# Scores that start 24 and 28 slots after their loads, and stores to scratch issued by ScalarE, in a hybrid attention and RG-LRU layer

## The chip, the cores and the metric

The kernel runs on one core of a Trainium2 chip. The metric is the device time of one execution in microseconds; lower is better. The core has a matrix engine (TensorE, "PE" in the profile, its weight loads "PEld"), a vector engine (VectorE, "DVE"), a scalar engine (ScalarE, "ACT"), a general engine (GpSimd, "POOL") and a queue engine that only issues transfers (SyncE, "SP"). Each engine runs its own instructions strictly in order and waits for the others on semaphores. Transfers (DMAs) run on 16 shared DMA engines; SP and ACT can issue them.

## What is computed

One decoder layer on 1024 positions of width 2048, in float32:

```
h = rms_norm(x, norm_gain)
q, k, v, g_attn, xr, g_rec = split(h @ w_in)         # 6 x 1024 columns
q, k = rope(q), rope(k)                              # 8 heads, 2 maps of 64 each
p = softmax(causal(q k^T / 8));  w = p[0] - lam * p[1]
o = rms_norm(w @ v, subln_gain) * (1 - lam_init) * silu(g_attn)
r = causal_conv(xr);  r = rg_lru(r) * silu(g_rec)    # 8 blocks of 128
x = x + concat(o, r) @ w_out
out = rms_norm(x, final_gain)
```

## The kernel before

The 1024 positions are worked off in two halves of 512 (`b` or `l` = 0 and 1). In each half, 16 units come in the order of `UNITS`: eight attention heads and eight recurrent blocks. A head unit makes four projections (the two halves of q and k, then v, then the gate), a recurrent unit two. One projection is 48 matmuls of 128x512 (16 row tiles of the input, 3 products each: every float32 operand is split into a high and a low part and high x high, high x low and low x high are added up); these are the matmuls of line 367. After the 16 units of a half comes the output projection (line 826).

Around this stream of projections the program places everything else by **slots**. The class `Slots` counts them: `tick()` moves the count by one, and generators (`stream`, `loader`, `scores`, `weighted`, `rope`, `values`, `lru`, `head_out`, stores) yield the number of slots until they go on. One slot passes for every three matmuls of a projection. So a `yield 4` puts what follows 12 matmuls later in TensorE's order. Slots set the order in which instructions are recorded, not times.

The weights come through `stream`: each 256 KB tile is loaded by SP into a raw buffer, ACT rounds it into the high part (line 169), POOL or DVE takes the low part (line 170). Buffers of 128x512 come from one pool of 89, first freed, first used again.

A head's way from projection to scores goes through scratch memory in HBM. When the second projection (pb) is done, DVE multiplies it by cosine and sine, `rope` subtracts and adds, splits into high and low, and four stores of 256 KB write the parts into the scratch tensor `fs`, whose first dimension has length 4 (each store has the shape 4 x 32 x 512). Then `head_load` reads it back in another arrangement: two k tiles (128x512) and four q tiles, each q tile a 64x512 block that is read twice (shape 2 x 64 x 512). In the second half also the k and v tiles of the first half are loaded. `scores` takes the head's tiles and issues, per block of 128 query rows, the score matmuls (line 632 with the high q, line 633 with the low q), the mask and maximum on DVE, the exponentials on ACT and the combination of both maps on DVE. `weighted` transposes the weights (line 755) and multiplies them with v (lines 777 to 780), `head_out` normalises.

Before the change, all transfers are issued by SP, through `load` (line 155) and `store` (line 159). The scores start three slots after their loads are recorded (`yield 3` in `scores`), and the loads are recorded one slot after the stores at the earliest (`yield 1` in `rope`).

In the texts below T0 is the moment at which TensorE finishes pb of a head.

Of the kernel before, what the change touches and what calls it, by code (L numbers as in the profile page):

```python
# [55 lines left out]
UNITS = ("h0", "h1", "r0", "h2", "r1", "h3", "r2", "h4", "r3", "h5", "r4", "h6", "h7", "r5", "r6",  # L56
         "r7")
ORDER = (0, 1, 2, 3, 4, 8, 9, 10, 11, 12, 5, 6, 13, 14, 7, 15)
SCORE_STEP = 2
SCORE_PACE = (4, 4)  # L60
TURN_PACE = 2
# [2 lines left out]
class Slots:  # L64


    def __init__(self):
        self.now = 0
        self.seq = 0
        self.tasks = []  # L70
# [36 lines left out]
class Trunk:  # L107
    def __init__(self, ctx, tc, io):
        self.tc = tc
        self.nc = tc.nc  # L110
        self.io = io
        e = ctx.enter_context
        self.cst = e(tc.tile_pool(name="cst", bufs=1))
        self.dram = e(tc.tile_pool(name="scr", bufs=1, space=bass.MemoryType.DRAM))
        self.bp = e(tc.tile_pool(name="buf", bufs=1))
        self.ps = e(tc.tile_pool(name="ps", bufs=1, space=bass.MemoryType.PSUM))
        self.tr, self.av, *self.dense = [
            self.ps.tile([P, HALF], F32, name=f"pq{i}") for i in range(4)]
        self.swide = [self.ps.tile([P, 1024], F32, name=f"sw{i}") for i in range(2)]
        self.n = 0  # L120
        self.sl = Slots()
        self.free = deque(range(NB))
        self.wide = [self.bp.tile([P, 1024], F32, name=f"wide{i}") for i in range(5)]
        self.avbusy = self.trbusy = False
        self.cur = self.phase = 0
        self.rsb, self.sin, self.cos, self.tabs, self.Y = {}, {}, {}, {}, {}
        self.fs, self.vsc, self.vnow, self.gate, self.rgate, self.msc = {}, {}, {}, {}, {}, {}
        self.ready, self.hd, self.es = set(), {}, {}
        self.scored, self.flipped, self.weighed = [], 0, 0

    def nm(self, s):
# [24 lines left out]

    def store(self, dst, b, delay=3, record=None, keep=False):
        def go():
            self.nc.sync.dma_start(dst, b.f)
            if record:  # L160
                record[0][record[1]] = dst
            if not keep:
                self.rel(b)
            return
            yield
        self.sl.spawn(go(), delay)
# [75 lines left out]
    def weights(self):  # L242
        io = self.io
        for b in range(2):
# [7 lines left out]
            yield from (io["w_in"][u, g] for u in us for g in range(4))  # L252
            yield from (io["w_out"][cg, kt] for cg in range(4) for kt in ORDER)

# [204 lines left out]
    def rope(self, b, h, ts):  # L459
        nc = self.nc  # L460
        t1, t2, t3, t4 = ts
        self.tt(t1.f, t1.f, t2.f, ALU.subtract)
        self.tt(t3.f, t3.f, t4.f, ALU.add)
        yield 1
        self.split(t1.f, t2, t1)
        self.split(t3.f, t4, t3)
        yield 4
        fs = self.dram.tile([4, 4, 32, HALF], F32, name=self.nm("fs"))
        for i, t in enumerate((t2, t4, t1, t3)):
            self.load(fs[:, i], t.f)  # L470
        self.rel(*ts)
        self.fs[h, b] = fs
        yield 1
        self.ready.add(("q", h, b))

    def values(self, b, h, vt):
        nc = self.nc
        yield 2
        while not self.settled():
            yield 1  # L480
        o = self.spare()
        for i in range(4):
            nc.tensor.transpose(o[:, i * P:(i + 1) * P], vt.f[:, i * P:(i + 1) * P], self.ident)  # L483
        vh, vl = self.allocr(), self.allocr()
        self.split(o, vh, vl)
        self.rel(vt)
        self.vnow[h] = (vh, vl)
        if b == 0:
            self.vsc[h] = (self.scratch("vs"), self.scratch("vs"))
            yield 4  # L490
            for d, t in zip(self.vsc[h], (vh, vl)):
                self.load(d, t.f)
        self.ready.add(("v", h, b))


# [88 lines left out]
    def head_load(self, h, l):  # L584
        k, q, v = [], [], []
        for c in range(l + 1):
            ks = []
            for m in range(2):
                kk = self.allocr()
                self.load(kk.f, self.fs[h, c][2 + m].rearrange("i r c -> (i r) c"))  # L590
                ks.append(kk)
            k.append(ks)
        for i in (0, 2):
            for m in range(2):
                t = self.allocr()
                src = self.fs[h, l][m, i:i + 2].rearrange("i r c -> (i r) c")
                self.load(t.f, src.unsqueeze(0).broadcast_to([2, 64, HALF]))
                q.append(t)
        if l:
            vs = []  # L600
            for d in self.vsc[h]:
                t = self.allocr()
                self.load(t.f, d)
                vs.append(t)
            v.append(vs)
        self.hd[h, l] = (k, q, v)

    def loader(self):
        for l in range(2):
            for h in range(NH):  # L610
                while (("q", h, l) not in self.ready or 8 * l + h - self.weighed > 1
                       or len(self.free) < FREE_HEAD):
                    yield 1
                self.head_load(h, l)
                yield 1

    def score(self, h, l, j, p0, es):
# [8 lines left out]
        for m in range(2):  # L626
            st = self.swide[m]
            for c in range((cols + 511) // 512):
# [4 lines left out]
                nc.tensor.matmul(o, lhsT=q[2 + m].r[:, qs], rhs=kk, start=False, stop=True)  # L633
        yield SCORE_STEP
        for m in range(2):
# [4 lines left out]
        nc.vector.tensor_scalar_mul(mx, mx, -(QK ** -0.5))  # L640
        yield SCORE_STEP
        p1 = self.wide[3]
        for m, p in enumerate((p0, p1)):
            nc.scalar.activation(p[:, :cols], self.swide[m][:, :cols], AF.Exp, scale=QK ** -0.5,  # L644
                                 bias=mx[:, m:m + 1], accum_out=sm[:, m:m + 1])
        yield SCORE_STEP
        nc.vector.tensor_tensor(out=es[:, j:j + 1], in0=sm[:, 0:1], in1=sm[:, 0:1], op=ALU.mult)
# [8 lines left out]
    def scores(self):  # L656
        n = 0
        for l in range(2):
            for h in range(NH):
                while (h, l) not in self.hd:  # L660
                    yield 1
                yield 3
                es = self.cst.tile([P, 4], F32, name=self.nm("es"), tag="es", bufs=4)
                self.es[h, l] = es
                for j in range(4):
                    while n - 2 * self.flipped > 3:
                        yield 1
                    p0 = self.wide[(0, 1, 2, 4)[n % 4]]
                    n += 1
                    yield from self.score(h, l, j, p0, es)  # L670
                    self.scored.append(p0)
                    yield SCORE_PACE[l]
                k, q, v = self.hd[h, l]
                self.rel(*q, *(t for ks in k for t in ks))
# [118 lines left out]
    def outputs(self, b):  # L793
# [10 lines left out]
        for cg in range(4):  # L804
            for i, kt in enumerate(ORDER):
                while cg == 0 and len(raws) + len(mixes) < min(KT, i + 5):
                    raws.append(self.mix(ORDER[len(raws) + len(mixes)], b))
                while cg == 0 and len(mixes) < min(KT, i + 2):
                    x, hi, lo = raws.popleft(), self.allocr(), self.allocr()
                    mixes[ORDER[len(mixes)]] = (hi, lo)  # L810
                    self.split(x.f, hi, lo)
# [55 lines left out]
            self.rel(y)  # L867

    def run(self):
        engines = {mybir.EngineType.PE, mybir.EngineType.SP}  # L870
        if True:
            self.consts()
            for gen in (self.stream(), self.loader(), self.scores(), self.weighted()):
                self.sl.spawn(gen)
            for b in range(2):
                for name in UNITS:
                    (self.head if name[0] == "h" else self.rec)(b, int(name[1]))
                self.final(b)
                self.outputs(b)
# [58 lines left out]
```

## Time and profile before

| | |
|---|---|
| time, median of 3 runs | 2202.98 us (2202.58 to 2203.88) |
| time of the profiled execution | 2201.42 us |
| its span, first to last instruction | 2199.6 us |
| TensorE busy | 1739.8 us (79%) |
| mean granted TensorE clock | 0.883 of full |
| ACT, POOL, DVE busy | 793.6, 858.7, 761.4 us |
| DMA engines' busy share (queue 1) | 34.2% |

A row of waits says which engine and line waited for what, and in how many pieces. The chain of waits follows the work that ended last back in time. In a table of windows the DMA share is the mean busy share of 16 DMA engines, so one engine alone is 0.0625. A "PEclk" of 0.50 is the lower of TensorE's two clocks (1.2 GHz) and 1.00 the higher (2.4 GHz). "b" is a buffer of the pool, "fs", "vs" and "ms" are scratch tensors in HBM (rotated q and k; v of the first half; gated outputs), "pq" and "sw" PSUM tiles.

### The profile page before, as it was taken

The numbers are of one execution on the slowest core, as the hardware profiler recorded it, in microseconds if no ns is written. First come the engines' busy times: TensorE is split into PE (matmuls) and PEld (weight loads), VectorE is DVE, ScalarE is ACT, GpSimd is POOL, SyncE is SP. The second block draws the span as 40 slices with busy tenths as digits, with TensorE's granted clock in tenths as the row PEclk, the third lists the DMA queues.
The fourth block names the chain that finished last, engine by engine and source line by source line (L and its number), as shares of the span: only waits on it lengthen the run. The fifth ranks groups of instructions, "written<-read, shape, count | busy, mean of one in ns | idle before, by whom it ended". The sixth has DMA issues, their size and how long they took to land. (4 is left out here: it accounts for less than half of the span.)

```text
span 2199.6 us, 22066 instructions
## 1 busy us (share of the span) xinstructions
PE 1739.8 (79%) x7716; PEld 1409.8 (64%) x7716; DVE 761.4 (35%) x1333; ACT 793.6 (36%) x1383; POOL 858.7 (39%) x710
## 2 busy tenths in 40 slices
PE   7568695959595869989957786959595958689996
PEld 5357474748484657778846675848484847577885
DVE  8334141515141335740223433324232424346001
ACT  6215151515151326642413342424251513266221
POOL 7313433424251325766613142415151513256560
PEclk9779897979797979999979897979797979799998
DMA  5423323233322234523723142423232323245422
GB/s 200 136 78 99 108 82 105 85 102 99 100 91 87 87 120 150 163 67 122 255 81 107 56 131 64 120 69 116 74 115 74 103 84 99 91 131 188 117 78 77
DMA packets 131503, 237.03 MB, mean 108 GB/s; under 512 B 13248, under 2 KB 17472, under 8 KB 131392
## 3 DMA queue, kind: packets, MB, share of 16 engines
q1 hardware_dynamic: 131392, 235.63, 34.2%
q8 instruction: 60, 0.98, 0.2%
q14 instruction: 51, 0.42, 0.1%
HBM read 197.83 MB, written 37.75 MB: 107 GB/s over the span
## 5 line engine op out<-in xcount | busy, mean ns | idle before, releaser
L367 PE MATMUL pq<-b,b 128*128 128x512 f32 x4512 | 1162.4, 410 | 17.2 <-ACT b L169 8.0
L170 POOL TENSOR_TENSOR b<-b,b 128x512 fp32r<-128x512 f32 x504 | 678.2, 1359 | 990.3 <-ACT b L169 706.6
L367 PEld LDWEIGHTS pq<-b,b 128*128 128x128 f32 x4512 | 877.5, 199 | 195.1 <-ACT b L169 8.5
L169 ACT CAST b<-b 128x512 fp32r<-128x512 f32 x592 | 349.7, 618 | 848.5 <-PE pq L367 219.6
L632 PE MATMUL sw<-b,b 128*128 128x512 f32 (+2 forms) x192 | 78.1, 408 | 278.1 <-DMA b<-fs 277.8
L173 DVE TENSOR_TENSOR b<-pq,b 128x512 f32<-128x512 f32 x113 | 75.1, 687 | 525.9 <-PE pq L367 434.6
L632 PEld LDWEIGHTS sw<-b,b 128*128 128x128 f32 x192 | 42.2, 220 | 296.3 <-issue 169.1
L637 DVE CUSTOM_DVE_ANT_0 sw<-sw,mask 128x128 f32<-128x128 f32 (+7 forms) x128 | 96.6, 770 | 376.2 <-PE sw L633 375.9
L826 PE MATMUL pq<-b,b 128*128 128x512 f32 x768 | 198.2, 393 | 5.0 <-DVE wide L173 5.0
L826 PE MATMUL sw<-b,b 128*128 128x512 f32 x768 | 196.3, 391 | 0.0
L826 PEld LDWEIGHTS pq<-b,b 128*128 128x128 f32 x768 | 144.9, 189 | 37.0 <-DVE wide L173 5.9
L826 PEld LDWEIGHTS sw<-b,b 128*128 128x128 f32 x768 | 145.3, 189 | 30.5
L173 POOL TENSOR_TENSOR b<-b,b 128x512 f32<-128x512 f32 (+1 forms) x98 | 129.4, 1325 | 89.8 <-ACT b L548 31.6
L633 PE MATMUL sw<-b,b 128*128 128x512 f32 (+2 forms) x192 | 77.1, 407 | 103.0 <-DMA b<-fs 103.0
L633 PEld LDWEIGHTS sw<-b,b 128*128 128x128 f32 x192 | 40.8, 212 | 126.8 <-DMA b<-fs 120.5
L644 ACT ACTIVATE wide<-sw,mx 128x128 f32<-128x128 f32 (+7 forms) x128 | 93.8, 738 | 67.0 <-DVE mx L640 66.2
L170 DVE TENSOR_TENSOR b<-b,b 128x512 fp32r<-128x512 f32 x88 | 92.1, 1071 | 32.5 <-ACT b L169 25.7
L169 ACT CAST b<-pq 128x512 fp32r<-128x512 f32 x16 | 9.4, 587 | 253.3 <-PE pq L483 253.3
L763 POOL MEMSET b<- 128x128 f32 x64 | 12.9, 205 | 185.0 <-PE pq L367 181.3
L764 ACT CAST b<-pq 128x512 fp32r<-128x512 f32 (+1 forms) x80 | 43.4, 542 | 108.5 <-PE pq L755 108.5
L765 DVE TENSOR_TENSOR b<-pq,b 128x512 fp32r<-128x512 f32 (+1 forms) x80 | 50.7, 634 | 45.1 <-ACT b L764 37.7
L755 PE MATMUL pq<-ident,wide 128*128 128x128 f32 x288 | 52.1, 286 | 17.6 <-DVE wide L652 16.8
(130 smaller groups left out, 1345.3 us busy)
## 6 DMA issues: line engine op xcount, KB each, us to landing
b<-w_in SPq DMA_DIRECT2D x384, 256.0 KB
b<-w_out SPq DMA_DIRECT2D x128, 256.0 KB
b<-fs SPq DMA_DIRECT2D x112, 256.0 KB
fs<-b SPq DMA_DIRECT2D x64, 256.0 KB
b<-xt SPq DMA_DIRECT2D x32, 256.0 KB
ms<-b SPq DMA_DIRECT2D x32, 256.0 KB
b<-ms SPq DMA_DIRECT2D x32, 256.0 KB
wide<-x SPq DMA_DIRECT2D x20, 256.0 KB
```

The source lines that it names most:

```text
L169: self.nc.scalar.copy(hi.r, x)
L170: (eng or self.nc.vector).tensor_tensor(out=lo.r, in0=x, in1=hi.f, op=ALU.subtract)
L173: (eng or self.nc.vector).tensor_tensor(out=out, in0=a, in1=b, op=op)
L367: self.nc.tensor.matmul(acc, lhsT=x.r[:, s], rhs=y.r, start=kt == 0 and j == 0, stop=kt == KT - 1 and j == 2)
L632: nc.tensor.matmul(o, lhsT=q[m].r[:, qs], rhs=kk, start=True, stop=False)
L633: nc.tensor.matmul(o, lhsT=q[2 + m].r[:, qs], rhs=kk, start=False, stop=True)
L637: nc.vector.tensor_tensor_reduce(out=s, in0=s, in1=self.mask[:, 896 - off:896 - off + cols], scale=1.0, scalar=NEG, op0=ALU.add, op1=ALU.m ...
L644: nc.scalar.activation(p[:, :cols], self.swide[m][:, :cols], AF.Exp, scale=QK ** -0.5, bias=mx[:, m:m + 1], accum_out=sm[:, m:m + 1])
L755: nc.tensor.transpose(self.tr[:, c:c + P], ws[qi][:, kb * P:(kb + 1) * P], self.ident)
L764: nc.scalar.copy(wh.r[:, first:], self.tr[:, first:])
L765: nc.vector.tensor_tensor(out=wl.r[:, first:], in0=self.tr[:, first:], in1=wh.f[:, first:], op=ALU.subtract)
L826: nc.tensor.matmul(accs[t], lhsT=x.r[:, s], rhs=z.r, start=i == 0 and j == 0, stop=i == KT - 1 and j == 2)
```

## The change

Three edits go together. The scores of a head now start 24 slots (first half) or 28 slots (second half) after its loads were recorded, instead of 3. In `rope` the loads can be recorded six slots after the stores instead of one. And the stores to scratch (four `fs` stores a head, two `vs` stores a head in the first half, one `ms` store for each head and block and half: 64 + 16 + 32 = 112 of them) are issued by ACT (`nc.scalar.dma_start`) instead of SP. The final stores of the output stay with SP. The deleted line in `run` was not used.

```diff
+SCORE_LEAD = (24, 28)
...
     def store(self, dst, b, delay=3, record=None, keep=False):
         def go():
-            self.nc.sync.dma_start(dst, b.f)
+            self.nc.scalar.dma_start(dst, b.f)
...
         for i, t in enumerate((t2, t4, t1, t3)):
-            self.load(fs[:, i], t.f)
+            nc.scalar.dma_start(fs[:, i], t.f)
         self.rel(*ts)
         self.fs[h, b] = fs
-        yield 1
+        yield 6
         self.ready.add(("q", h, b))
...
             for d, t in zip(self.vsc[h], (vh, vl)):
-                self.load(d, t.f)
+                nc.scalar.dma_start(d, t.f)
...
         self.hd[h, l] = (k, q, v)
+        self.loaded[h, l] = self.sl.now
...
                 while (h, l) not in self.hd:
                     yield 1
-                yield 3
+                while self.sl.now < self.loaded[h, l] + SCORE_LEAD[l]:
+                    yield 1
```

How TensorE's order changes is seen at head 3 of the second half. Before, where its first score matmuls stand (sw_70 and sw_71 are the score tiles of the two maps, b_9318 and b_9320 k tiles, b_9326 and b_9328 the high q tiles, pq_69 and pq_68 projections):

```order
L367 MATMUL pq_69<-b_6144,b_9273 128x512
L367 MATMUL pq_69<-b_6145,b_9273 128x512
L632 MATMUL sw_70<-b_9318,b_9326 128x512
L367 MATMUL pq_69<-b_6144,b_9274 128x512
L367 MATMUL pq_69<-b_6166,b_9273 128x512
L367 MATMUL pq_69<-b_6167,b_9273 128x512
L632 MATMUL sw_71<-b_9320,b_9328 128x512
L367 MATMUL pq_69<-b_6166,b_9274 128x512
L367 MATMUL pq_68<-b_5710,b_9301 128x512
```

The same place now (lines are shifted by one to three; b_9347 and b_9349 are the high, b_9351 and b_9353 the low q tiles):

```order
L368 MATMUL pq_69<-b_5941,b_9426 128x512
L368 MATMUL pq_69<-b_5940,b_9427 128x512
L634 MATMUL sw_70<-b_9339,b_9347 128x512
L635 MATMUL sw_70<-b_9339,b_9351 128x512
L634 MATMUL sw_70<-b_9343,b_9347 128x256
L635 MATMUL sw_70<-b_9343,b_9351 128x256
L634 MATMUL sw_71<-b_9341,b_9349 128x512
L635 MATMUL sw_71<-b_9341,b_9353 128x512
L634 MATMUL sw_71<-b_9345,b_9349 128x256
L635 MATMUL sw_71<-b_9345,b_9353 128x256
L368 MATMUL pq_69<-b_5970,b_9444 128x512
```

The first score matmul stood behind 44 projection matmuls after pb of its own head; now it stands behind 120 of them and the four transposes of v. In the first half (head 3) these numbers are 49 and 108. The eight score matmuls of a block now stand together.

On ACT, before, the place where the head's rotated q and k are rounded (b_9117 and b_9119 are the high parts):

```order
L169 CAST b_9491<-b_9313 128x512
L169 CAST b_9117<-b_9116 128x512
L169 CAST b_9119<-b_9118 128x512
L169 CAST b_9525<-b_9351 128x512
L169 CAST b_9588<-b_9383 128x512
```

And now (b_9005 and b_9007 are the high parts, b_9226 the gated output of the head before):

```order
L170 CAST b_9444<-b_9313 128x512
L160 DMA ms_9263<-b_9226 128x512
L170 CAST b_9005<-b_9004 128x512
L170 CAST b_9007<-b_9006 128x512
L471 DMA fs_9305<-b_9005 4x32x512
L471 DMA fs_9305<-b_9007 4x32x512
L471 DMA fs_9305<-b_9004 4x32x512
L471 DMA fs_9305<-b_9006 4x32x512
L170 CAST b_9460<-b_9331 128x512
```

One store of `ms` stands ahead of the two casts, and the four stores of `fs` ahead of the next rounding of weights. On SP, the loads of the head stood behind its four stores and one weight load; now they stand behind weight loads only, with one weight load among them (b_9347 to b_9353 are the q tiles, b_9343 and b_9345 the k tiles):

```order
L156 DMA b_9433<-w_in 128x512
L156 DMA b_9347<-fs_9305 128x1x512
L156 DMA b_9349<-fs_9305 128x1x512
L156 DMA b_9472<-w_in 128x512
L156 DMA b_9343<-fs_9305 128x512
L156 DMA b_9345<-fs_9305 128x512
L156 DMA b_9351<-fs_9305 128x1x512
L156 DMA b_9353<-fs_9305 128x1x512
L156 DMA b_9494<-w_in 128x512
```

## Rows read from the trace of the kernel before

**Rows 1.** The page: span, busy time of the engines, and the granted TensorE clock and the DMA share in 40 slices (in tenths).

```profile
span 2199.6 us, 22066 instructions
PE 1739.8 (79%) x7716; PEld 1409.8 (64%) x7716; DVE 761.4 (35%) x1333; ACT 793.6 (36%) x1383; POOL 858.7 (39%) x710
...
PEclk9779897979797979999979897979797979799998
DMA  5423323233322234523723142423232323245422
```

**Rows 2.** Who waited for whom, TensorE's two longest: engine, tile and line, what it waited for, total us, times, longest us.

```profile
PE sw L632 <- DMA b<-fs: 277.8, 24, 19.2
...
PE sw L633 <- DMA b<-fs: 103.0, 32, 5.3
```

**Rows 3.** The chain that ended last, in order of time, around head 3 of the second half: start us, us, what.

```profile
1399.74 19.09 PE pq L367 x84
1419.47 1.94 DVE b L173 x2
1424.21 12.63 DMA fs<-b
1436.92 2.61 SPq L155
1440.85 19.39 DMA b<-fs
```

**Rows 4.** The timeline around the same head: start us, us, engine, line, operation, tiles, count, and in brackets the idle time before and what ended it.

```profile
1414.81 13.99 PE L367 MATMUL pq<-b,b 128*128 128x512 f32 x61
...
1418.86 1.29 DVE L173 TENSOR_TENSOR b<-pq,b 128x512 f32<-128x512 f32 x2 [9.59 <-PE pq L367]
...
1421.43 1.23 ACT L169 CAST b<-b 128x512 fp32r<-128x512 f32 x2 [1.95 <-DVE b L173]
1422.08 3.34 SPq L155 DMA_DIRECT2D fs<-b  x4
1425.52 2.72 SPq L155 DMA_DIRECT2D b<-w_in  x1
1431.21 14.96 SPq L155 DMA_DIRECT2D b<-fs  x6
...
1443.31 0.76 PE L632 MATMUL sw<-b,b 128*128 128x512 f32 x1 [14.51 <-DMA b<-fs]
...
1446.21 5.17 SPq L155 DMA_DIRECT2D b<-w_a  x1
...
1448.38 0.80 PE L632 MATMUL sw<-b,b 128*128 128x512 f32 x1 [3.03 <-DMA b<-fs]
...
1455.22 0.50 PE L633 MATMUL sw<-b,b 128*128 128x512 f32 x1 [2.52 <-DMA b<-fs]
...
1460.29 0.79 PE L633 MATMUL sw<-b,b 128*128 128x512 f32 x1 [3.54 <-DMA b<-fs]
```

**Rows 5.** Windows in the same stretch: window, us, busy us of PE, PEld, DVE, ACT and POOL with counts, granted clock, DMA share, GB/s.

```profile
1424.00:1428.00 4.00, 4.00 (x20) 3.30 (x19) 0.00 (x0) 0.00 (x0) 0.21 (x1) 1.00 0.24 62
...
1432.00:1436.00 4.00, 0.00 (x0) 0.00 (x0) 0.00 (x0) 1.14 (x2) 1.54 (x2) 0.50 0.26 99
1436.00:1440.00 4.00, 0.00 (x0) 0.00 (x0) 0.00 (x0) 0.00 (x0) 1.14 (x2) 0.50 0.14 53
...
1444.00:1448.00 4.00, 1.35 (x4) 0.53 (x2) 0.00 (x0) 0.62 (x1) 0.00 (x0) 0.50 0.13 50
...
1456.00:1460.00 4.00, 0.75 (x3) 0.15 (x2) 0.89 (x2) 0.00 (x0) 0.00 (x0) 0.50 0.12 46
1460.00:1464.00 4.00, 3.71 (x11) 3.22 (x12) 1.75 (x4) 1.81 (x5) 0.63 (x1) 0.50 0.01 5
1464.00:1470.00 6.00, 6.00 (x27) 4.82 (x25) 3.57 (x9) 1.86 (x5) 1.10 (x2) 0.85 0.18 44
```

**Rows 6.** The timeline around head 3 of the first half, columns as in rows 4.

```profile
329.79 26.68 PE L367 MATMUL pq<-b,b 128*128 128x512 f32 x117
...
345.40 1.29 DVE L173 TENSOR_TENSOR b<-pq,b 128x512 f32<-128x512 f32 x2 [9.59 <-PE pq L367]
...
348.39 3.14 SPq L155 DMA_DIRECT2D fs<-b  x4
...
375.09 0.55 PE L632 MATMUL sw<-b,b 128*128 128x256 f32 x1 [18.62 <-DMA b<-fs]
...
386.41 0.58 PE L633 MATMUL sw<-b,b 128*128 128x256 f32 x1 [3.68 <-DMA b<-fs]
```

**Rows 7.** Timeline rows at the higher clock for the small matmuls: three transposes of weights, two neighbouring products with v, and one 512-column score matmul beside its neighbour (columns as in rows 4).

```profile
395.21 0.55 PE L755 MATMUL pq<-ident,wide 128*128 128x128 f32 x3
...
398.16 0.28 PE L777 MATMUL pq<-b,b 128*128 128x256 f32 x1
398.28 0.28 PE L779 MATMUL pq<-b,b 128*128 128x256 f32 x1
...
405.70 0.39 PE L632 MATMUL sw<-b,b 128*128 128x512 f32 x1
405.93 0.39 PE L633 MATMUL sw<-b,b 128*128 128x512 f32 x1
```

**Rows 8.** SP's own waits before it could issue: the stores of `ms`, and transfers that waited for an ACT cast (total us, times, longest us).

```profile
SPq L155 <- ACT b L169: 101.5, 23, 20.8
...
SPq L159 <- POOL b L173: 62.5, 32, 9.2
```

**Rows 9.** A window in the output projection of the first half, columns as in rows 5.

```profile
1000.00:1110.00 110.00, 106.55 (x471) 87.91 (x469) 19.73 (x36) 37.97 (x73) 59.39 (x48) 1.00 0.57 185
```

More of the change, by code (lines that the diff above doesn't have):

```diff
@@ L127, in __init__ @@
         self.fs, self.vsc, self.vnow, self.gate, self.rgate, self.msc = {}, {}, {}, {}, {}, {}
-        self.ready, self.hd, self.es = set(), {}, {}
+        self.ready, self.hd, self.es, self.loaded = set(), {}, {}, {}
         self.scored, self.flipped, self.weighed = [], 0, 0
@@ L869, in run @@
     def run(self):
-        engines = {mybir.EngineType.PE, mybir.EngineType.SP}
         if True:
```

## The prediction

> **What bounds the kernel now.** I read the page first. TensorE is busy 1739.8 of 2199.6 us and no other engine is busy above 39% [rows 1], so the time is TensorE's work plus its waits. The list of waits then shows that almost all of TensorE's idle time has one cause: score matmuls that wait for the tiles loaded back from `fs`, 277.8 us at line 632 and 103.0 us at line 633, together 380.8 of the 459.8 us idle [rows 2]. The dips of the granted clock to 0.7 in the slices [rows 1] are the same places. The chain, taken in order of time, gives the order of one head: projection, rotation, 12.63 us of stores to `fs`, 2.61 us of SP issuing, 19.39 us of loads from `fs`, scores [rows 3].
>
> The timeline gives the distances. In head 3 of the second half T0 is 1418.86 (DVE starts on pb). The first store is issued at T0 + 3.2, the first load at T0 + 12.4, and the four q tiles land one after another at 1443.31, 1448.38, 1455.22 and 1460.29: the last at T0 + 41.4 [rows 4]. TensorE ran out of work at 1428.8. In head 3 of the first half T0 is 345.40, stores are issued at T0 + 3.0 and the last q tile has landed at T0 + 41.0 [rows 6]. So the chain from T0 to the last q tile is 41 us in either half.
>
> What makes it so long stands in the windows. While the stores run, the DMA share is 0.24 and 0.26, which is 4 engines of 16; while the q tiles are loaded it is 0.14, 0.13 and 0.12, which is 2 of 16 [rows 5]. The first dimensions of the two shapes are 4 and 2. A q tile takes 5.07 us there (1443.31 to 1448.38, 1455.22 to 1460.29; the two k tiles lie in the 6.84 between) [rows 4]. The chain is bandwidth on the few engines that these transfers use, hardly waiting in queues.
>
> **The change part by part.**
>
> *Longer lead.* At the higher clock 84 projection matmuls take 19.09 us [rows 3], 0.2273 us each. TensorE used to reach the first score 49 x 0.2273 = 11.1 us after T0 (first half) or 44 x 0.2273 = 10.0 us (second half). Now 108 and 120 of them and four transposes of v (0.18 us each after the transposes of rows 7, 0.7 together) stand ahead: 25.2 and 28.0 us. The chain needs 41. So most waits shrink to about 16 and 13 us and do not go. What a head gains is the work that TensorE has behind it when the last q tile lands. Before, in the first half: 49 projection matmuls and 8 more that stood between the first scores, 57. After: 108, and 0.5 us of transposes more. Gain (108 - 57) x 0.2273 + 0.5 = 12.1 us. Second half: 44 + 13 = 57 before, 120 after, 14.3 us; 0.5 more for transposes, less four score matmuls of the block that before were already done (0.8 us): 14.0.
>
> The wait that stays still lets the clock fall: it was 0.50 in windows from 1432 to 1464 and back within the next [rows 5]. The scores and matmuls behind the wait run at the lower clock in both kernels, so this cancels.
>
> Four heads have more cover, since the head before ends only 64 slots earlier and part of its attention now lies between pb and the scores. Head 1, first half: 132 projection matmuls, where 63 + 8 were done before, 13.9 us, and 12 score matmuls and 3 transposes more, 2 us: 16. Head 7, first half: 7 transposes, 12 products with v at 0.12 us, 4 scores and the head's normalisation, 5 us more [rows 7]: 17. Heads 1 and 7 of the second half: 36 products (4.3), 15 transposes (2.8), 8 scores (1.8) and normalisation (1.3), 10 us more: 24 each. Their cover is 38 us, so some 3 us of wait stay.
>
> Sum: first half 10.5 (head 0, which had 54 matmuls already) + 5 x 12.1 + 16 + 17 = 104; second half 6 x 14.0 + 2 x 24 = 132. Together 236 us.
>
> *Stores from ACT.* The 112 stores leave SP. What was behind them there, loads that SP could not issue, was not late: TensorE has no large wait for weights in the list. On ACT the four stores cost what they cost on SP, 3.3 us a head [rows 4], in an engine that is 36% busy [rows 1]. Behind them stand roundings of weights that TensorE uses 130 and more matmuls later (30 us), so this is hidden; if it were not, it would cost at most 16 x 3.3 = 53 us. The `ms` store of the head before now stands ahead of the two casts that feed the `fs` stores. SP waited 62.5 us for POOL before 32 such stores, 2.0 us on average and 9.2 at the longest [rows 8]. On ACT this puts the casts back by about 1 us, since they themselves become ready 2 us after T0: 16 us lost, bounds 0 and 16 x 9.2 = 147. Against that, the weight loads ahead of the head's loads wait for nothing later than 13 matmuls before T0; before, two stood between T0 and the first load, and each takes its part of the slow engines' time: a store takes 12.63 / 4 = 3.2 us on 4 engines, so the same 256 KB spread over 16 take 0.8 us of each. That gives back 1.6 us a head, 26 us. I take the two as cancelling.
>
> The trace shows one queue only. By its rows the chain is as long as stores and loads keep the same few engines busy: four stores in 12.63 us, four q tiles in 20.3, and nothing gained by splitting them over two queues. The Trainium skill says the same against this part of the change (DMA: Bandwidth & Descriptors, Issuing engines are not separate DMA queues): transfers begun by several engines run on the same 16 DMA engines, and beginning them elsewhere saves only the time of issuing. By that rule the stores from ACT are worth nothing here and the 236 us stand; the shares of rows 5 agree, but no row here has a second queue.
>
> *Six slots instead of one.* The loads stand 5 slots (3.4 us) later in SP's order, but they wait for the stores until T0 + 12.4 anyhow. Nothing.
>
> *Weights.* TensorE now runs on during the loads, and weight loads issued behind the q tiles share their two engines: they land after T0 + 41. They belong to tiles used 200 and more matmuls after T0, 20 us after the scores. In the output projection the stream carries TensorE at 97% with a DMA share of 0.57 [rows 9].
>
> Profiled execution: 2201.4 - 236 = 1965.4. The median of the runs is 1.6 us above it: 1967.
>
> **The rivals.**
>
> *A second queue runs beside the first.* If stores from ACT and loads from SP did not stand behind each other on the slow engines, the first q tile, issued at T0 + 12.4, would land 6.4 us later (as it now does from 1436.92, when the stores are done, to 1443.31) and not at T0 + 24.4; the last then 17.0 later (1443.31 to 1460.29), at T0 + 35.8. Another 5.6 us in 14 heads, 3 in two: 84 us, 1883. For it: no row shows two queues. Against it: the share stays at 0.26 while the first loads are already issued [rows 5].
>
> *The wait goes wholly.* The remaining waits are 6 x 16 + 5 + 10 in the first half and 6 x 13.4 + 2 x 3 in the second, 197 us: 1770. It needs a chain of 25 to 28 us; the four q tiles alone take 20.3.
>
> *Weights or casts become late.* ACT issues the `vs` stores of the first half (T0 + 14) and waits there for earlier transfers, among them q and k tiles that land at T0 + 30; behind them stand roundings of weights. If these are needed sooner than I count, the eight heads of the first half lose their gain: 1967 + 104 = 2071. Against it: the tiles that TensorE uses up to 190 matmuls after T0 are rounded ahead of these stores.
>
> *Slower: ACT reaches the `fs` stores late.* ACT is in order; SP, which did nothing else, waited up to 20.8 us for an ACT cast and up to 9.2 for POOL [rows 8]. Every microsecond by which the stores are late moves the chain's end by one in 16 heads. It decides from 236 / 16 = 14.8 us a head; at 20.8 it is 16 x 20.8 - 236 = 97 us slower, 2300. Against it: ACT cast the head's tiles at T0 + 2.6 [rows 4].
>
> **How the numbers follow.** My forecast 0.60 (1967, own range 1930 to 2020 by the bounds of the ACT and weight terms), second queue 0.16, wait gone 0.06, weights late 0.14, slower 0.04. The range that holds 8 in 10 leaves out the slower case, the vanished wait and the far end of the weights: 1870 to 2070. About 0.2% (4.4 us) is what a measurement of this kernel can tell from no change: faster 0.95, same 0.01, slower 0.04.
>
> **What would show it.** Right: the wait of TensorE for loads of `fs` falls from 380.8 to some 190 us, with single waits of 8 to 16 us in most heads, none in the products with v; the store chain still near 12.6 us at a DMA share of 0.25 and the q tiles 5 us apart at 0.13; the q tiles' landing still at T0 + 41. Wrong: a wait of TensorE for ACT or POOL at line 368 (weights), a landing clearly before T0 + 38 or after T0 + 45, or stores issued by ACT later than T0 + 6.

## The result, and the profile after

The changed kernel takes 2098.47 us (median of 4 runs, 2093.89 to 2101.67), the kernel before 2202.78 us beside it: a ratio of 0.9524, 95% interval 0.9512 to 0.9536, 104 us faster. The direction was forecast, the size was not: 1967 us were forecast, with 1870 to 2070 as range. The profiled execution has a span of 2098.7 us, 100.9 us less than before, so 135 of the 236 us forecast are missing.

The page of the changed kernel, its lines for the span, the engines' busy time and the granted clock:

```profile
span 2098.7 us, 22044 instructions
PE 1724.3 (82%) x7716; PEld 1408.4 (67%) x7716; DVE 779.1 (37%) x1333; ACT 804.7 (38%) x1393; POOL 849.8 (40%) x710
PEclk9879989898898889999989898989898999899998
```

Beside [rows 1] TensorE is busy 15 us less (less work at the lower clock) and idle 374.4 us instead of 459.8. ACT has ten instructions more: 113 instead of 103 loads of its function tables, 1.28 us each. Who TensorE waited for now (total us, times, longest us):

```profile
PE sw L635 <- DMA b<-fs: 83.8, 17, 9.3
PE pq L368 <- DVE b L171: 64.0, 7, 12.3
PE pq L758 <- DVE wide L654: 63.2, 22, 5.4
PE pq L726 <- ACT b L723: 44.1, 3, 14.8
PE sw L634 <- DMA b<-fs: 33.2, 6, 8.8
...
PE pq L737 <- DVE hs L734: 8.7, 2, 7.8
```

The wait for `fs` fell from 380.8 us [rows 2] to 117.0, further than the 190 forecast. But 180 us stand at places that had 18 us before: a projection that waits for a spare PSUM tile to write into (line 368), the transposes of the weights for the products with v (758), the normalisation of a head (726, 737). Nearly all of the 18 us stood at the transposes:

```profile
PE pq L755 <- DVE wide L652: 16.8, 20, 3.1
```

What is behind the waits shows in ACT's waits, after and before:

```profile
ACT b L170 <- DMA b<-w_in: 390.5, 40, 25.7
```

```profile
ACT b L169 <- DMA b<-w_in: 57.8, 14, 19.9
```

The timeline of head 3 of the second half, the place of [rows 4]; T0 is 1360.23:

```profile
1360.23 1.28 DVE L174 TENSOR_TENSOR b<-pq,b 128x512 f32<-128x512 f32 x2
...
1363.69 2.42 ACTq L471 DMA_DIRECT2D fs<-b  x4
...
1373.25 1.16 SPq L156 DMA_DIRECT2D b<-fs  x2
1375.82 4.38 SPq L156 DMA_DIRECT2D b<-w_in  x1
1380.29 7.92 SPq L156 DMA_DIRECT2D b<-fs  x4
...
1390.15 0.62 ACT L170 CAST b<-b 128x512 fp32r<-128x512 f32 x1 [17.33 <-DMA b<-w_in]
1390.67 0.58 ACT L170 CAST b<-pq 128x512 fp32r<-128x512 f32 x1
...
1391.28 0.69 DVE L171 TENSOR_TENSOR b<-pq,b 128x512 fp32r<-128x512 f32 x1 [19.88 <-ACT b L170]
...
1392.03 7.34 PE L368 MATMUL pq<-b,b 128*128 128x512 f32 x24 [10.00 <-DVE b L171]
...
1402.63 0.80 PE L635 MATMUL sw<-b,b 128*128 128x512 f32 x1 [2.35 <-DMA b<-fs]
```

The stores begin at T0 + 3.5, the loads at T0 + 13.0, and the last q tile has landed at T0 + 42.4: the chain is as long as before, a microsecond longer. The wait is elsewhere. ACT stands 17.33 us at a weight tile that lies among the q loads on SP. Behind it, in ACT's order, stands the cast of v, which reads the PSUM tile that TensorE's next projection needs; so TensorE stands still for 10 us, until 1392.03, and at the scores only 2.35 us of wait are left for q. The clock falls in this wait, as in [rows 5] (columns as there):

```profile
1368.00:1372.00 4.00, 4.00 (x19) 3.32 (x18) 0.69 (x1) 1.36 (x3) 0.39 (x2) 1.00 0.26 99
...
1388.00:1392.00 4.00, 0.00 (x0) 0.00 (x0) 0.72 (x2) 1.62 (x3) 0.09 (x1) 0.50 0.13 51
...
1400.00:1404.00 4.00, 1.65 (x6) 1.26 (x5) 1.00 (x3) 0.62 (x1) 0.01 (x1) 0.79 0.13 51
```

The DMA share is 0.26 during the stores and 0.13 during the q loads, 4 engines and 2, as before. Later in the same head TensorE waits at the transposes, 18 projection matmuls behind the last scores:

```profile
1443.26 0.62 ACT L170 CAST b<-b 128x512 fp32r<-128x512 f32 x1 [3.60 <-DMA ms<-b]
...
1446.56 1.28 DVE L654 SCALAR_TENSOR_TENSOR wide<-wide,mx,wide 128x1024 f32<-128x1024 f32 x1
1447.90 0.90 PE L758 MATMUL pq<-ident,wide 128*128 128x128 f32 x3 [5.41 <-DVE wide L654]
```

The exponential comes late on ACT: here behind a cast into a buffer that an `ms` store, now in ACT's own stream, still reads. Head 3 of the first half, the place of [rows 6], T0 336.02:

```profile
336.02 1.29 DVE L174 TENSOR_TENSOR b<-pq,b 128x512 f32<-128x512 f32 x2 [6.55 <-PE pq L368]
...
338.60 0.53 ACTq L471 DMA_DIRECT2D fs<-b  x1
339.69 2.74 ACTq L471 DMA_DIRECT2D fs<-b  x3
...
365.13 0.55 PE L634 MATMUL sw<-b,b 128*128 128x256 f32 x1 [4.18 <-DMA b<-fs]
372.81 0.58 PE L635 MATMUL sw<-b,b 128*128 128x256 f32 x1 [7.13 <-DMA b<-fs]
377.96 0.58 PE L635 MATMUL sw<-b,b 128*128 128x256 f32 x1 [4.36 <-DMA b<-fs]
...
393.11 0.55 PE L758 MATMUL pq<-ident,wide 128*128 128x128 f32 x3 [1.30 <-DVE wide L654]
```

TensorE reaches the scores at T0 + 25 and waits 4.18 + 7.13 + 4.36 = 15.7 us for q: here the forecast of 16 held.

The time between the T0 of heads (the DVE rows) shows where the gain is missing, in us:

| stretch | before | after | gain | forecast |
|---|---|---|---|---|
| start to T0 of head 0 | 71.6 | 74.9 | -3.2 | 0 |
| first half, heads 0 and 1 | 166.2 | 159.3 | 7.0 | 26.5 |
| heads 2 to 5 | 428.6 | 404.8 | 23.8 | 48.4 |
| heads 6 and 7, to the second half's head 0 | 430.9 | 421.7 | 9.2 | 29.1 |
| second half, heads 0 and 1 | 206.9 | 191.5 | 15.4 | 38.0 |
| heads 2 to 5 | 458.6 | 435.6 | 23.0 | 56.0 |
| heads 6 and 7, to the end | 436.7 | 410.9 | 25.8 | 38.0 |

The eight single heads miss 57.6 us, the four pairs (two heads with no recurrent unit between) 74.2.

### The profile page after: what moved, and what is told of

Same layout as the page of the kernel before. It is cut to its first block, busy times and chain, and to the rows that moved or that the text cites. A ratio compares the mean times of both kernels' runs of the same rounds, so it can differ in the third digit from the quotient of the medians.

```text
span 2098.7 us, 22044 instructions
## 1 busy us (share of the span) xinstructions
PE 1724.3 (82%) x7716; PEld 1408.4 (67%) x7716; DVE 779.1 (37%) x1333; ACT 804.7 (38%) x1393; POOL 849.8 (40%) x710
## 4 chain that ended last, share of the span: by engine, by line
PE 31%; DMA 14%; DVE 7%; ACT 3%; issue 2%; SPq 2%; POOL 1%; ACTq 0%; POOLq 0%; DVEq 0%
PE pq L368 11%; PE pq L829 8%; PE sw L829 8%; DMA fs<-b 5%; DMA b<-fs 4%; DMA b<-w_in 4%; SPq L156 2%; DVE b L174 2%; DMA ms<-b 1%; PE pq L758 1%; DVE sw L639 1%; ACT wide L646 1%; DVE b L533 1%; ACT b L170 1%; DVE wide L654 1%
## 5 line engine op out<-in xcount | busy, mean ns | idle before, releaser
L829 PEld LDWEIGHTS sw<-b,b 128*128 128x128 f32 x768 | 145.6, 190 | 30.6
L635 PE MATMUL sw<-b,b 128*128 128x512 f32 (+2 forms) x192 | 70.7, 377 | 83.8 <-DMA b<-fs 83.8
L758 PE MATMUL pq<-ident,wide 128*128 128x128 f32 x288 | 56.0, 304 | 66.9 <-DVE wide L654 63.2
L634 PE MATMUL sw<-b,b 128*128 128x512 f32 (+2 forms) x192 | 69.4, 367 | 40.5 <-DMA b<-fs 33.2
L635 PEld LDWEIGHTS sw<-b,b 128*128 128x128 f32 x192 | 38.4, 200 | 94.3 <-DMA b<-fs 88.9
L455 DVE SCALAR_TENSOR_TENSOR b<-b,b 128x512 f32<-128x512 f32 x32 | 31.1, 971 | 178.0 <-ACT b L453 178.0
L758 PEld LDWEIGHTS pq<-ident,wide 128*128 128x128 f32 x288 | 38.0, 154 | 85.9 <-DVE wide L654 73.0
L634 PEld LDWEIGHTS sw<-b,b 128*128 128x128 f32 x192 | 38.2, 199 | 49.2 <-issue 30.3
```

Source lines behind the costliest of these rows:

```text
L634: nc.tensor.matmul(o, lhsT=q[m].r[:, qs], rhs=kk, start=True, stop=False)
L758: nc.tensor.transpose(self.tr[:, c:c + P], ws[qi][:, kb * P:(kb + 1) * P], self.ident)
L829: nc.tensor.matmul(accs[t], lhsT=x.r[:, s], rhs=z.r, start=i == 0 and j == 0, stop=i == KT - 1 and j == 2)
```

## The experiments

The first theory, A: the gain is given back because loads queued on SP behind the q loads come late, and ACT waits for them in order. Rivals: B, the stores on ACT hold ACT up; C, the transfers on few engines are the only limit.

**Each half of the change alone.** `lead_only` puts the stores of all three kinds back on SP (one of the three places is shown); `stores_only` keeps them on ACT and takes the lead back.

```diff
-            nc.scalar.dma_start(fs[:, i], t.f)
+            self.load(fs[:, i], t.f)
```

> The changed kernel with its stores back on SP's queue; the longer lead of the loads stays. Theory A (part of the hidden time is given back: weight tiles queued on SP behind the q loads come late, ACT waits in order for them, and the casts, exponentials and copies behind those waits make TensorE wait): the queue of the stores plays no part, so about the time of the changed kernel, 2098 us, within 20. Theory B (what is missing was lost to the stores on ACT: its issues and its waits for their landings hold ACT up): 1990 us or less, the forecast nearly whole. Theory C (the transfers of q over few DMA engines are the only limit left): as A, 2098.

Measured: 2129.0 us, ratio 0.9667 (0.9651 to 0.9684). So the stores on ACT did not cost the missing gain (B falls); with the long lead they brought 31 us.

```diff
-SCORE_LEAD = (24, 28)
+SCORE_LEAD = (3, 3)
...
-        yield 6
+        yield 1
```

> The stores on ACT's queue with the old, short lead of the loads over the scores. A: 2200 us, within 10 of the kernel before, since a store from the other queue shortens nothing on the chain from the end of a projection to the last q tile (41 us). B: slower than before, 2230 us or more. If instead the second queue is what brought the 104 us, about 2100.

Measured: 2219.1 us, ratio 1.0076 (1.0061 to 1.0091): alone the stores on ACT cost 17 us, 1 us a head. In single heads the first load goes out at T0 + 13.4 to 14.3 instead of T0 + 12.3 to 12.6 (second half). A second queue has nothing to run beside: the q loads wait until the stores of their head have landed, whichever engine issued these. SP's wait for the landings in the changed kernel (99.9 us before):

```profile
SPq L156 <- DMA fs<-b: 187.8, 34, 10.4
```

The Trainium skill (DMA: Bandwidth & Descriptors, Issuing engines are not separate DMA queues) has transfers begun by several engines run on the same 16 DMA engines; the ratio of 1.0076 agrees in that another issuing engine saved no time. The 31 us are explained below.

**The q loads over all engines.**

```diff
-                self.load(t.f, src.unsqueeze(0).broadcast_to([2, 64, HALF]))
+                for r in (0, 64):
+                    self.load(t.f[r:r + 64, :], src)
```

> The changed kernel with each load of a q tile (128x512, read through a broadcast, on 2 of 16 DMA engines) made as two loads of 64x512 of the same source. If these spread over more engines, the four q tiles land in some 3 us instead of 20, the chain to the last q tile ends some 15 us earlier, and weight tiles no longer stand behind slow loads. A: both the waits for q (117 us in the sum) and those for late casts (some 200 us) go in good part: about 1850 us. C: only the 117 go: about 1980. B: about 1980 too, with ACT's waits for the landings of its stores left as they are. If the loads take the same two engines as before: 2098.

Measured: 1849.6 us, ratio 0.8395 (0.8380 to 0.8410), 249 us under the changed kernel. Its waits of TensorE and a window while a head's loads run (T0 is 1183.06, the loads are issued from 1195.65):

```profile
PE pq L759 <- DVE wide L655: 60.1, 22, 5.5
...
PE sw L636 <- DMA b<-fs: 10.8, 11, 2.1
```

```profile
1204.00:1208.00 4.00, 4.00 (x19) 3.30 (x18) 0.69 (x1) 0.00 (x0) 3.15 (x3) 1.00 0.83 261
```

The share is 0.83 instead of 0.13, the waits for q are 11 us instead of 117, and the waits that stood at lines 368, 726 and 737 fell with them from 116.8 to 5.8 us; of the 180 us only the transposes' wait is left. Of the gain 32 us are less busy time of TensorE (1691.9 us, less work at the lower clock), the rest less idle. The slow q loads are the root, as A has it, and C falls short. The Trainium skill has the rule (DMA: Bandwidth & Descriptors, Rules for kernel authors): a leading broadcast dimension of c copies keeps a transfer on at most c engines; the shares 0.13 and 0.83 agree.

The same edit in the kernel before, and in the longer lead with the stores on SP:

> The kernel before (short lead, stores on SP), each q load made as two of 64x512. The first runs gave the changed kernel with this edit 1850 us. If the number of DMA engines that a q tile uses is the cause of the wait, the chain of 41 us ends 16 to 17 us earlier and the wait of a head falls from 25 to some 8 us: 2202 - 16 x 16 = 1946 us. If the split works only through the longer lead (as cover for the weight tiles behind it): above 2100. If the lead is worth nothing once the q tiles are fast: 1850.

Measured: 1915.1 us, ratio 0.8691 (0.8677 to 0.8705). Single heads wait 8.3 to 8.8 us for q, at T0 + 19 to 20 instead of T0 + 41. The time is 31 us below the 1946 expected, which counted the waits alone: TensorE is also busy 43 us less (1696.6 us). The edit alone is worth 288 us, more than the whole change, and the longer lead is then still worth 65 to 72.

> Longer lead, stores on SP's queue, q loads split. With slow q loads the stores on ACT were worth 31 us (2129 against 2098). If these 31 us came from weight tiles and stores that share SP's queue with slow loads, they go when the loads are fast: 1850 us, within 10. If ACT's queue as such is better (a store that waits for its cast no longer holds up SP's loads), 1875 to 1885.

Measured: 1843.1 us, ratio 0.8382 (0.8349 to 0.8415), no slower than with the stores on ACT. So ACT's queue has its worth only beside slow q loads.

**Weights rounded later.**

```diff
-WRING = 4
-WAHEAD = 6
+WRING = 3
+WAHEAD = 8
```

> The changed kernel with its weight tiles rounded later after their load (ring of ready tiles 3 instead of 4, loads 8 tiles ahead instead of 6), so that a tile that lies behind the q loads is asked for later by ACT; the transfers of q stay as they are. A: ACT's waits for weight tiles (390 us) and with them TensorE's waits for spare PSUM tiles, for exponentials and for head copies (some 200 us) shrink to about half: about 2000 us. C and B: 2098, within 20, as nothing on the transfers or the stores has changed. If the smaller ring of ready tiles makes the weights themselves late, above 2098 with waits of TensorE at the weight loads.

Measured: 2083.1 us, ratio 0.9459 (0.9441 to 0.9476): 15 us, where A expected 98. TensorE's waits for the spare tile are gone (head 3 of the second half now waits 10.0 and 3.8 us for q, together 13.8 where it waited 12.4), and by their T0 the eight single heads take 6 us longer, while the pairs gain 18. In a single head the stall at line 368 only stood in the place of the wait for q: A in its first form falls there.

**Transposes later.** A second theory, D: the missing gain is at the transposes, whose exponentials now fall among the recurrent unit's work.

```diff
+                    yield 8
                     ws = self.scored[at:at + 2]
```

> The changed kernel with the transposes of a head's weights 8 slots (24 projection matmuls, 5.5 us) later after the last score block; nothing else. Theory D, formed after the first runs: with the longer lead the exponentials of a head fall into the work of a recurrent unit on ACT and DVE (table loads of 1.28 us between them), so the transposes, 18 matmuls behind the scores as before, wait for them: 63 us of TensorE's waits that before were 17. The wait then falls to under 20 us, and the time to about 2055 us. Rival: the products with v are only where a lateness of ACT shows; it then shows at the next place (the head's normalisation or the recurrent unit's matmuls) and the time stays at 2098, within 10.

Measured: 2094.4 us, ratio 0.9505 (0.9491 to 0.9519), no gain to speak of, though the wait for line 654 fell from 63.2 to 6.2 us. The timeline, head 3 of the second half, T0 at 1347.81:

```profile
1353.92 1.73 ACTq L471 DMA_DIRECT2D fs<-b  x3
...
1392.45 0.80 PE L635 MATMUL sw<-b,b 128*128 128x512 f32 x1 [4.09 <-DMA b<-fs]
```

The last three stores are begun at T0 + 6.1 to 7.3 instead of T0 + 4.1 to 5.3, and the last q tile lands at T0 + 44.6 instead of 42.4. In single heads the chain took back what the transposes gave. Elsewhere, in the pairs above all, the wait moved on, as the rival had it, to places behind the copies of the transposed weights, which had 3.7 and 0.7 us in the changed kernel:

```profile
PE pq L759 <- DVE b L769: 46.6, 11, 15.2
...
PE pq L781 <- ACT b L768: 30.1, 3, 19.4
```

This run does not price the transposes' wait; with fast q loads the next one does:

> Both edits, q loads split and transposes 8 slots later, on the changed kernel. Theory D: the 60 us that TensorE waits for the weights of the products with v in the split kernel go too: about 1805 us. Rival as for the later transposes alone: 1850, within 10.

Measured: 1831.3 us, ratio 0.8323 (0.8308 to 0.8339): 18 us, of the 45 that D expected; part moved on, to the recurrent gates (26.5 us at line 545, from 19.7) and to the copies of the transposed weights (18.9 us at line 760, from 1.9).

**A shorter lead.**

```diff
-SCORE_LEAD = (24, 28)
+SCORE_LEAD = (16, 17)
```

> The changed kernel with leads of 16 and 17 slots instead of 24 and 28. If a head's time is the landing of the last q tile (T0 + 42) plus TensorE's work behind it plus the waits of the products with v: the wait for q grows by 5.5 us in the first half and 7.5 in the second, the waits of the products shrink by at most 2.8 and 5.3, so about 2130. If the longer lead itself is what costs (exponentials among the recurrent unit's work), 2080 or less.

Measured: 2153.2 us, ratio 0.9777 (0.9757 to 0.9796), even above the accounting's 2130. The long lead itself is not what costs.

> Changed kernel, q loads split, leads 16 and 17. With the short lead the split kernel waits 8.7 us a head for q, which is 38 matmuls or 13 slots; 16 slots cover it. Theory D (the exponentials of a long lead meet the recurrent unit's work): 30 to 45 us of the 60 us of waits in the products go, about 1815. If the lead has no part in them: 1850.

> As the last, with the stores on SP's queue. With the long lead and split loads SP's queue was 7 us faster than ACT's (1843 against 1850). If ACT's queue is only of use while q loads are slow: 1805 to 1815, no slower than the run with ACT's stores.

Measured: 1894.9 us (0.8601, 0.8584 to 0.8618) and 1883.0 us (0.8553, 0.8534 to 0.8572). Both expectations were missed: 45 and 40 us slower than with the long lead. By the T0 of the heads, the first loses 40 us in the pairs and 10 in the single heads of the first half (2.5 each), and gains 11 in those of the second (2.7 each), where alone D holds. A single head of the first half waits in sum about as long as with the long lead (7.5 us on average, 7.4 there), but for q and at one place. Its windows:

```profile
321.00:325.00 4.00, 0.55 (x1) 0.29 (x1) 0.00 (x0) 0.00 (x0) 0.48 (x1) 0.74 1.00 294
325.00:329.00 4.00, 2.13 (x6) 1.70 (x7) 0.89 (x5) 0.00 (x0) 0.00 (x0) 0.50 0.92 280
329.00:333.00 4.00, 4.00 (x11) 3.14 (x10) 0.16 (x1) 3.85 (x8) 1.28 (x1) 0.50 0.19 73
333.00:337.00 4.00, 4.00 (x18) 3.23 (x18) 2.99 (x5) 1.26 (x2) 1.29 (x1) 0.98 0.00 0
```

From 329 to 333 TensorE is busy throughout and makes 11 matmuls, at the lower clock; from 333 to 337 it makes 18. By the granted clock of the four windows the lower level lasts some 10 us (2.1 + 4 + 4 + 0.2). Waits of 2.0 and 1.3 us lie in it, so some 6.8 us are work at half the clock, about 3 us lost.

**Loads taken out from behind q.** The third theory, E: A holds for the pairs, where more than the wait for q is lost, through any load that SP issues behind the q loads.

```diff
-WAHEAD = 6
+WAHEAD = 10
```

> The changed kernel with weight tiles loaded up to 10 ahead of their rounding instead of 6: about four tiles that stood behind a head's q loads on SP now stand ahead of them. Theory E: in heads that follow each other without a recurrent unit between (heads 0 and 1, 6 and 7, in both halves) the gain was lost to weight tiles that land behind the q loads and hold up ACT (stores of head 1, copies of the normalisation, 14.8 us each). Then the 64 us of waits at the projections and the 44 us at the normalisation go, and the pairs give 40 us or more: 2055. In plain heads nothing is won, since there the wait for q comes back in the place of the wait for the spare tile. If late weight tiles are not the cause: 2098, within 10.

Measured: 2068.8 us, ratio 0.9391 (0.9369 to 0.9412), 30 us. The waits for the spare tile and at line 726 are gone. But by the T0 of the profiled execution the pairs gain 18.4 us, where E expected 40 or more, and the eight single heads 18.7, where it expected none. In single heads of either half the transposes now wait 2.5 us, where they waited 4.4 and 5.3, so late tiles had a part in that wait too:

```profile
PE pq L758 <- DVE wide L654: 35.6, 14, 4.4
```

The second half's pairs wait 13 us at line 737. The timeline shows what comes next behind the q loads:

```profile
1144.39 0.87 SPq L156 DMA_DIRECT2D b<-w_x  x1
...
1153.54 0.40 ACT L526 CAST b<-b 128x256 fp32r<-128x256 f32 x1 [14.82 <-DMA b<-w_x]
...
1155.72 2.08 PE L737 MATMUL pq<-ident,hs 128*128 128x128 f32 x8 [13.29 <-DVE hs L734]
```

ACT waits 14.82 us for the gate weights of the next recurrent unit, and the root for the normalisation stands behind that cast. So these were loaded before the head's projections as well (the place in `head` is shown; the recurrent unit then loads them only where they are missing):

```diff
...
+        if (b, nxt) not in self.raws:
+            self.raw_gate(b, nxt)
         ts = [self.alloc() for _ in range(4)]
...
```

> The changed kernel with weight tiles loaded up to 10 ahead, and the gate weights of the next recurrent unit loaded before the projections of the head in front of it instead of behind that head's q loads. Theory E (loads queued behind q hold up ACT, in pairs of heads above all): ACT's waits for gate weights (134 us) go, and with them TensorE's 28 us at the normalisation in three pairs; about 2040. If these waits only stand in the place of the wait for q: 2069, within 8.

Measured: 2045.5 us, ratio 0.9286 (0.9272 to 0.9299), near the 2040 that E expected; no row of waits at the normalisation above 2 us is left. By T0 the pairs gain 34.8 us on the changed kernel, the single heads 13.4 (all of it in the first half), the start 3.8.

> Longer lead alone, stores on SP, weight tiles loaded up to 10 ahead. With 6 ahead, ACT's queue for the stores was worth 31 us (2129 against 2098). If that is because stores on SP delay the weight loads behind them, it goes with the deeper lookahead: 2069, within 10. If the second queue moves the stores or the q tiles themselves sooner: about 2100.

Measured: 2063.5 us, ratio 0.9369 (0.9354 to 0.9384), level with ahead10. So the 31 us of ACT's queue were the same cause: stores that stand on SP ahead of weight loads made these later still. ACT's wait for them in lead_only:

```profile
ACT b L170 <- DMA b<-w_in: 458.8, 42, 29.2
```

**All together.**

> All together on the changed kernel: q loads split, weight tiles 10 ahead, gate weights early, transposes 8 slots later; stores on ACT. Split loads with later transposes gave 1831. If what is left there (27 us at the gates' matmuls, 19 and 13 at the products, 10 at a normalisation) is lateness of ACT behind late tiles: 1805. If not: 1831, within 8.

> The same with the stores on SP's queue. With split loads and the long lead SP's queue was level or 7 us ahead (1843 against 1850): 1800 to 1810 if that holds; if stores on SP delay the loads behind them also here, 1825 or more.

Measured: 1807.8 us (0.8199, 0.8185 to 0.8213) and 1799.7 us (0.8166, 0.8154 to 0.8178). The second is the fastest version, 299 us under the changed kernel, with the stores on SP. TensorE is busy 93% of its span of 1795.0 us:

```profile
PE 1667.9 (93%) x7716; PEld 1367.8 (76%) x7716; DVE 793.6 (44%) x1333; ACT 815.2 (45%) x1400; POOL 864.4 (48%) x710
```

## Why the prediction was right in direction and wrong in size

- **What bounds the kernel: right.** The chain of 41 us, the 4 engines of the stores and the 2 of the q tiles stand in the changed kernel as before, and the split q loads show that the 2 engines are the cause of the waits. The 4 engines of the stores were not varied.
- **The work ahead of the last landing: 1.5 to 1.75 us a head too high.** Work before the landing is its distance from T0 less the waits for q. First half, mean of heads 2 to 5: 41.0 - 25.25 = 15.75 before, 42.5 - 16.2 = 26.3 after, 10.55 more where 12.1 were forecast. Second half, with the wait for the spare tile: 41.4 - 23.4 = 18.0 and 42.7 - 12.45 = 30.25, 12.25 where 14.0 were forecast. The step counted projection matmuls at the higher clock; in the old order the matmuls and scores between the waits ran at the lower and took their time too.
- **The landing: 1.5 and 1.3 us later**, at T0 + 42.5 and 42.7. Of the two effects that the step on the stores let cancel, only the loss of 1 us was there (stores_only).
- **"None in the products with v": wrong, the largest term in single heads.** The transposes' wait rose by 2.8 us a head in the first half (4.4 from 1.6) and by 5.3 in the second (from 0). The prediction moved the scores and did not look at what ACT and DVE do in the new place. Together 1.5 + 1.5 + 2.8 = 5.8 of the 6.2 us that a head misses in the first half, 1.75 + 1.3 + 5.3 = 8.35 of 8.25 in the second.
- **"Weights: used 20 us after the scores": the step that failed.** It asked when TensorE needs the tiles, and not what stands behind their cast on ACT. ACT's wait for weight tiles rose from 58 to 390 us; behind it stood the casts that free the spare tile, the copies and the root of the normalisation. The sign that the prediction named for it, a wait of TensorE for ACT or POOL at line 368, stayed at 8 us; the wait came by way of DVE (64.0 us). In single heads the stall at the spare tile took only the place of the wait for q, and late tiles cost what they added to the transposes' wait. In the pairs they ate the extra cover: of the 74 us missing there 35 came back with ahead10_gate, and of the 135 missing in all 52. The 39 that remain in the pairs, 5 us a head, are no more than single heads still miss.
- **Stores from ACT, "worth nothing": wrong beside slow loads.** They were worth 31 us, as relief of SP's queue ahead of the weight loads, and nothing once these came early or q was fast.
- **The rivals.** "Weights or casts become late" was the right kind, put at 0.14 with 2071 us and in the wrong place: not at the `vs` stores of the first half but at SP's loads behind q, in both halves. The second queue could not run beside the first, since the loads wait for the landing of the stores; the prediction, which argued from the DMA share, did not see this wait. "ACT reaches the `fs` stores late" came true in head 1 of the first half (T0 101.16), by way of DVE: the rounding that the last store needs stands there behind the mask of head 0's scores, and these wait for q.

```profile
130.43 0.30 DVE L639 CUSTOM_DVE_ANT_0 sw<-sw,mask 128x128 f32<-128x128 f32 x1 [9.70 <-PE sw L635]
...
130.64 0.69 DVE L171 TENSOR_TENSOR b<-b,b 128x512 fp32r<-128x512 f32 x1
```

```profile
131.36 0.53 ACTq L471 DMA_DIRECT2D fs<-b  x1
```

The store is begun at T0 + 30, since a lead that is counted in slots lets head 0's scores pass behind head 1's projections.

Not settled: how much of the transposes' wait is the recurrent unit's work and how much late tiles. Loading ahead took it from 4.4 to 2.5 us a head in the first half and from 5.3 to 2.5 in the second. With early gate weights it was 1.8 in the first half, but 4 again in the second, and late_turn moved the stores with it.

## What to carry to other kernels

Before a wait is covered with other work, look at the transfer that makes it: a load over 2 of 16 engines showed as a DMA share of 0.13, and two loads of half the rows were worth 288 us where hiding it was worth 104. Work that is pulled into a wait needs its own inputs there: list every load queued behind the slow one, and for each the first instruction that stands behind its consumer on an in-order engine. A wait that goes is only gone when the next one behind it is priced too.

## What was not expected of the hardware

A queue engine is itself held by slow transfers ahead. SP's issue of one weight tile between the q loads took 4.38 us (the row at 1375.82 above), and the profile shows no wait in it. The issue of such a tile (least, median and most, in ns) took, over the changed kernel and over split_q:

```profile
L156 SPq DMA_DIRECT2D b<-w_in x384: 327/328/7052, 1.6 to 1851.7; - x192
```

```profile
L156 SPq DMA_DIRECT2D b<-w_in x384: 327/328/1242, 1.6 to 1603.3; - x192
```

Some of the long issues hold a wait for a buffer as well; those without one reach 6.75 us. So loads behind the slow ones are begun late as well as landed late.

And waits of 2.5, 2.0 and 1.3 us in a row took the granted clock to 0.50 for some 10 us (split_q_lead16), as one long wait does: what a wait costs is more than its length.
